# A hybrid trunk step: sums for the FFN's seven products formed ahead and in place, buffers kept through both FFN stages

## The chip, the cores and the metric

The kernel runs on one core of one Trainium2 chip. The time is that of one execution on the device, in microseconds (us), from three runs and one profiled execution. The engines of the core are TensorE (PE in the rows, its weight loads PEld), VectorE (DVE), ScalarE (ACT), GpSimd (POOL) and SyncE (SP), which issues nearly all DMAs. Each has its own queue of instructions, taken in order.

## The reference

One layer of a trunk: a token mixer (three head groups and one output projection), then a SwiGLU FFN, each with normalisation before and after. 2048 latent tokens and 256 context tokens pass, 1024 wide. The change touches the end of the mixer and the FFN; D_FF is 2816.

```python
def rmsnorm(x, g):
    y = xf * lax.rsqrt(jnp.mean(xf * xf, axis=-1, keepdims=True) + EPS)
    return (y * g.astype(jnp.float32)).astype(x.dtype)
...
    m, extra = mixer(h)
    x = x + gt1 * rmsnorm(m, g_norm[1])
    h = rmsnorm(x, g_norm[2]) * (1.0 + sc2) + sh2
    gate, up = jnp.split(h @ w_gu, 2, axis=-1)
    f = (jax.nn.silu(gate) * up) @ w_down
    x = x + gt2 * rmsnorm(f, g_norm[3])
```

## The kernel before

All matrices are fp32, and each product is made of three: an operand is split into a high part, rounded by ScalarE, and a low part, the rest, formed by VectorE (`split`, L1694 to L1696), and TensorE multiplies high by high, high by low and low by high. The 2304 tokens are 18 tiles of 128 (tiles 0 to 15 latent, 16 and 17 context) or six groups of 384.

**Output stage** (`phase_out`). For each tile TensorE makes the 48 matmuls of the output projection into `m`. Then come the residual (a ScalarE sum of squares L1671, two small GpSimd steps, VectorE L1673 and L1674) and the second norm (ScalarE L1606, VectorE `xn` L1608). `store` turns `xn` by eight transposes in four PSUM buffers `pst`, ScalarE evicts them with scale and shift (L1623), and a DMA writes them to `h2`. `store` of a tile comes two tiles later; the last two come after the loop. `ffn_ahead` loads the first operands of the FFN during the loop: the splits of two quarters of h (`hop0`, `hop1`), the raw half `hr1` and the first weights `wr0`.

**Up stage** (`ffn_up`). Three token blocks of 768 tokens, 22 units each. A unit makes 128 columns of gate and of up for a block. The 2 × 2 × 2 blocks (gate and up, two halves of the 1024 inputs, two token groups) are multiplied with seven products instead of eight, by sums of operands: products 1 and 2 add into PSUM buffer X, products 6, 7 and 4 into Y, 5 and 3 into Z. Each product is 12 matmuls of 128 × 384, so a unit has 84. `prep_h` forms the operands of h for a block, in two halves of 768 columns: four sums (two on VectorE, L1750 to L1758, two on GpSimd, L1762 and L1768) and the splits `hop`. `prep_w` loads the weights of a unit by three DMAs (`w_raw`), forms four sums S on GpSimd (L1786 to L1789) and splits seven operands `gop` from a pool of ten. Partial results leave X, Y and Z through ScalarE (`p1` L1809, silu L1826, L1831) and VectorE (`u2` L1814, `u3` L1820 and L1821, L1828, L1830); GpSimd makes the two last products (L1829, L1832), and six DMAs write `a`. TensorE runs the end of a unit (products 4 and 3) after the first product of the next.

**Down stage** (`ffn_down`). Two halves of 512 output columns, each 18 tiles of 22 row blocks with three matmuls of 128 × 512. `a_load` reads and splits half a tile's `a` (raw `ar`, split `ao`, three buffers each), `w_load` the 22 weight blocks (raw `wr`, four buffers; split `wd`, 24). All its buffers are opened when those of the up stage are closed. In each half the weights are loaded row by row while tile 0 runs.

**Order.** TensorE runs in the order of the code (`InOrder`, L31 to L42), and so does SyncE in the output stage. The order on VectorE, ScalarE, GpSimd, and SyncE in the FFN, is set by the tile scheduler, by priority and by when buffers come free.

## Time and profile before

| | us |
|---|---|
| three runs | 3836.85, 3842.79, 3843.37 |
| median | 3842.79 |
| profiled execution | 3837.47 |
| its span | 3835.5 |
| TensorE busy | 3607.6 (94%) |
| VectorE busy | 2308.8 (60%) |
| ScalarE busy | 1723.1 (45%) |
| GpSimd busy | 966.3 (25%) |

Busy times are sums over the span. The output stage ends at 2217 us, the up stage at 3251 us, and the down stage lasts to the end. The mean granted TensorE clock of the span is 0.974 of full. Line numbers are those of the kernel before; a name such as `hop` stands for all buffers of that name, and what was read stands right of `<-`.

### The profile page before, as it was taken

The page shows a single profiled execution, that of the slowest core. Times are in us where ns is not written, and L with a number is a line of the kernel's source. Part 1 is how long each engine was busy: PE and PEld are TensorE (multiplying, and loading weights), DVE is VectorE, ACT ScalarE, POOL GpSimd, SP SyncE. Part 2 cuts the span into 40 slices and gives each one's busy share as a digit, 9 for nine tenths or more (in the row PEclk, how much of TensorE's full clock was granted, in tenths as well). Part 3 has the DMA queues.
Part 4 walks back from the last instruction along what each step waited for, and adds up shares of the span by engine and source line. Part 5 has one row for each costly group of instructions (what it writes and reads, how often), then busy time and mean ns, then how long its engine had stood idle before and what let it go on. Part 6 is the DMA issues. An engine that isn't in the chain of part 4 may idle for free. (4 is left out here: it accounts for less than half of the span.)

```text
span 3835.5 us, 64839 instructions
## 1 busy us (share of the span) xinstructions
PE 3607.6 (94%) x24526; PEld 3166.5 (83%) x24526; DVE 2308.8 (60%) x4786; ACT 1723.1 (45%) x3552; POOL 966.3 (25%) x1135
## 2 busy tenths in 40 slices
PE   8997999969999999989999969999999998899999
PEld 5887988956777777778878869999999998688787
DVE  4784477689655555568765576677667664322433
ACT  4223322236666666657865643343334333322221
POOL 0002322620000000000003355556555553000111
PEclk9998999989999999999999989999999999899999
DMA  7565877741211112255325643333333332633654
GB/s 270 200 210 175 259 223 225 197 116 48 55 48 51 44 46 52 64 160 144 90 79 186 213 132 99 98 108 108 105 93 97 101 96 75 208 111 125 194 187 133
DMA packets 649081, 501.15 MB, mean 131 GB/s; under 512 B 253681, under 2 KB 577120, under 8 KB 646464
## 3 DMA queue, kind: packets, MB, share of 16 engines
q1 hardware_dynamic: 645984, 493.41, 42.9%
q8 instruction: 193, 3.16, 0.4%
q10 hardware_dynamic: 2624, 3.55, 0.3%
q14 instruction: 120, 0.98, 0.1%
q0 software_dynamic: 160, 0.05, 0.0%
HBM read 348.14 MB, written 148.73 MB: 130 GB/s over the span
## 5 line engine op out<-in xcount | busy, mean ns | idle before, releaser
L37 PE MATMUL pd<-wd,ao 128*128 128x512 f32 x2376 | 550.3, 394 | 26.1 <-DMA wr<-in_w_down_dram 15.0
L37 PEld LDWEIGHTS pd<-wd,ao 128*128 128x128 f32 x2376 | 450.6, 190 | 125.7 <-ACT ao L1695 15.4
L37 PE MATMUL Y<-hop,gop 128*128 128x384 f32 x2376 | 452.3, 338 | 22.4 <-ACT hop L1695 9.8
L1034 ACT ACTIVATE PT<-pt 128x512 f32<-128x512 f32 (+1 forms) x600 | 331.9, 553 | 256.3 <-PE pt L37 249.4
L37 PEld LDWEIGHTS Y<-hop,gop 128*128 128x128 f32 x2376 | 422.1, 191 | 24.2 <-ACT hop L1695 10.1
L1696 DVE TENSOR_TENSOR gop<-S,gop 128x512 fp32r<-128x512 f32 x264 | 235.6, 893 | 167.3 <-ACT gop L1695 157.6
L37 PE MATMUL X<-hop,gop 128*128 128x384 f32 x1584 | 306.2, 342 | 18.7 <-DVE hop L1696 8.9
L37 PE MATMUL po<-PT,V 128*64 128x256 f32 (+1 forms) x3072 | 313.5, 341 | 2.2 <-ACT PT L1034 1.9
L37 PE MATMUL pso<-whi,hi 128*128 128x384 f32 (+2 forms) x864 | 288.8, 334 | 25.3 <-ACT whi L255 13.8
L37 PEld LDWEIGHTS X<-hop,gop 128*128 128x128 f32 x1584 | 283.5, 190 | 20.8 <-DVE hop L1696 9.6
L37 PE MATMUL pt<-ident,P 128*128 128x128 f32 x1752 | 284.9, 280 | 14.9 <-ACT PT L1034 7.9
L37 PE MATMUL Z<-hop,gop 128*128 128x384 f32 x1584 | 297.7, 336 | 0.0
L37 PE MATMUL pso<-whi,lo 128*128 128x384 f32 (+2 forms) x864 | 282.6, 327 | 7.6 <-DMA lo<-hl 7.6
L37 PE MATMUL pso<-wlo,hi 128*128 128x384 f32 (+2 forms) x864 | 282.9, 327 | 0.8 <-DVE wlo L256 0.5
L37 PEld LDWEIGHTS Z<-hop,gop 128*128 128x128 f32 x1584 | 278.7, 189 | 0.1
L37 PEld LDWEIGHTS pt<-ident,P 128*128 128x128 f32 x1752 | 200.3, 141 | 94.4 <-ACT PT L1034 36.3
L1695 ACT ACTIVATE gop<-S 128x512 fp32r<-128x512 f32 x264 | 166.2, 630 | 228.2 <-PE Y L37 124.9
L971 POOL TENSOR_TENSOR rSe<-rS,eh 64x128 f32<-64x128 f32 x144 | 55.0, 400 | 811.6 <-DVE rS L1003 780.9
L1696 DVE TENSOR_TENSOR gop<-wr,gop 128x512 fp32r<-128x512 f32 x198 | 200.9, 1015 | 83.8 <-ACT gop L1695 77.6
L37 PEld LDWEIGHTS po<-PT,V 128*64 128x64 f32 x3072 | 180.4, 136 | 79.3 <-issue 33.7
L1695 ACT ACTIVATE gop<-wr 128x512 fp32r<-128x512 f32 x198 | 125.2, 632 | 245.3 <-PE Z L37 174.7
L1696 DVE TENSOR_TENSOR ao<-ar,ao 128x1408 fp32r<-128x1408 f32 x72 | 127.4, 1769 | 145.1 <-ACT ao L1695 143.1
(323 smaller groups left out, 7208.1 us busy)
## 6 DMA issues: line engine op xcount, KB each, us to landing
ar<-a SPq DMA_DIRECT2D x72, 704.0 KB, 4.8
wr<-in_w_gu_dram SPq DMA_DIRECT2D x66, 512.0 KB, 4.1
wr<-in_w_gu_dram SPq DMA_DIRECT2D x132, 256.0 KB, 3.4
a<-o SPq DMA_DIRECT2D x396, 64.0 KB, 2.1
wm<-in_w_mod_dram SPq DMA_DIRECT2D x48, 512.0 KB, 4.1
hi<-hh SPq DMA_DIRECT2D x36, 512.0 KB, 5.4
lo<-hl SPq DMA_DIRECT2D x36, 512.0 KB, 6.4
st<-ptk SPq DMA_DIRECT2D x18, 768.0 KB, 4.1
```

The lines of the kernel that those rows point to most:

```text
L37: r = f(*x, **kw)
L971: nc.gpsimd.tensor_tensor(Se[hh[x], d], S[hh[x], d, :, hh[x]], e.unsqueeze(2).to_broadcast([64, 2, 64]), ALU.mult)
L1034: self.nc.scalar.activation(out, p, AF.Copy)
L1695: self.nc.scalar.activation(hi, raw, AF.Copy)
L1696: self.nc.vector.tensor_tensor(lo, raw, hi.bitcast(F32), ALU.subtract)
```

## The change

The sums of h for the first block are formed in the output stage (`ffn_ahead`, tiles 12 to 15), in whole width (1536 columns) and in place: `ht` and the two halves of `hr1`. The first two weight operands are split at tiles 16 and 17. The last tile's norm goes into a kept buffer (`xn_last`), and its transposes, evictions and store move into the first unit, behind product 5. The weight sums S go from GpSimd to VectorE (`w_sums`). The weight operands use eight buffers, six of tag `raw` and two of tag `y` of the pool `o_p`, which now stays open through both FFN stages; `feed` makes an operand as soon as the product eight before has been issued. At a change of block each h operand is replaced, in place, behind its last product in the block's last unit (`h_put`), in one split of 1536 columns; the sums for the next block are written in units 12 to 16 of the running one (`ahead`). Products of a unit after the first run in the order 1, 6, 5, 2, 7, 4, 3, as before.

For the down stage, `feed` goes on with eight operands of w_down in the same buffers; two halves of `a` are loaded into the halves of `hr1` and split into the buffers of `ht` and `hop0`. A ring of four (`ht`, the two of `hop0`, one more) holds the `a` operands after that, two raw buffers feed it. Tiles 0 and 1 of each half run as a pair, row by row; the weights for the second half are loaded row by row while the last tile of the first half runs. All pools of the FFN release buffers tile by tile. `phase_out` has two buffers for transposes and shares two more, which the up stage and the first pair of down use after it.

```diff
+            pst = es.enter_context(tc.tile_pool(name="o_t", bufs=2, space=PSUM))
             psm = es.enter_context(tc.tile_pool(name="o_m", bufs=2, space=PSUM))
-            pst = es.enter_context(tc.tile_pool(name="o_t", bufs=4, space=PSUM))
+            banks = [pst, self.xps]
...
-                xn = nt[t] = wk.tile([128, 1024], F32, tag="xn", name="xn", bufs=3)
-                sq = wk.tile([128, 1024], BF16, tag="sq2", name="sq2", bufs=1)
+                xn = self.raw() if t == NT - 1 else wk.tile([128, 1024], F32, tag="xn", name="xn", bufs=3)
+                nt[t] = xn
...
-            store(NT - 1)
+            self.xn_last = nt.pop(NT - 1)
...
+        self.ht = pool.tile([128, 2, 4, BT], F32, name="ht", tag="ht")
+        self.fe = pool
...
             self.w_raw(0, self.wr0)
+            tt(self.ht[:, 0], self.hr1[:, 0:4], hop[:, 0].bitcast(F32), ALU.subtract)
+        if t == 13:
+            tt(self.ht[:, 0], self.ht[:, 0], hop[:, 1].bitcast(F32), ALU.subtract)
+        if t in (14, 15):
+            self.h_sums(t - 13)
+        if t >= NT - 2:
+            n = t - NT + 2
+            self.gops[0, n + 1] = self.g_op(self.wr0[:, n + 1])
+    def h_sums(self, i):
+        tt = self.nc.vector.tensor_tensor
+        B12, B22 = self.hr1[:, 0:4], self.hr1[:, 4:8]
+        if i == 1:
+            tt(self.ht[:, 1], B22, self.ht[:, 0], ALU.subtract)
+        else:
+            tt(B12, B22, B12, ALU.subtract)
...
+        x = self.yraw() if self.gn % 8 < 2 else self.raw()
+        self.gn += 1
+        return x.bitcast(F32R).rearrange("p (s x) -> p s x", s=2)
+    def g_op(self, x):
+        w = self.g_buf()
+        self.split(w[:, 0], w[:, 1], x)
+        return w
...
-            gp = es.enter_context(tc.tile_pool(name="u_g", bufs=10))
-            rp = es.enter_context(tc.tile_pool(name="u_r", bufs=2))
...
+            H = {n: hp.tile([128, 2, 4, BT], F32R, name=f"hop{n}") for n in (6, 5, 7, 4, 3)}
...
+            def h_load(tb, j):
+                self.sp.dma_start(hx, self.h2_d[2 * tb][:, 4 * j:4 * j + 4])
+            def h_put(tb, n):
+                if n == 4:
+                    tt(ht[:, 1], hx, ht[:, 1], ALU.subtract)
+                x = {1: hx, 2: hx, 3: hr1[:, 4:8], 4: ht[:, 1], 5: ht[:, 0], 6: ht[:, 1], 7: hr1[:, 0:4]}[n]
+                self.split(H[n][:, 0], H[n][:, 1], x)
+                if n == 1:
+                    h_load(tb, 1)
...
+            def w_sums(u):
+                A21, A11, A12, A22 = [wr[u % 2][:, i] for i in range(4)]
+                S = [wk.tile([128, 512], F32, tag="S", name="S", bufs=4) for _ in range(4)]
+                tt(S[0], A21, A22, ALU.add)
+                tt(S[1], S[0], A11, ALU.subtract)
+                tt(S[2], A11, A21, ALU.subtract)
+                tt(S[3], A12, S[1], ALU.subtract)
+                return {1: A11, 6: S[1], 5: S[0], 2: A12, 7: S[2], 4: A22, 3: S[3]}
+            made, done, raws = [2], set(), {}
...
+                    elif m >= 8 and m - 8 not in done:
+                        return
...
+                    if u >= NU:
+                        if self.down_feed(m - 7 * NU):
+                            return
...
-                gp_.tensor_tensor(S[0], A21, A22, ALU.add)
-                gp_.tensor_tensor(S[1], S[0], A11, ALU.subtract)
-                gp_.tensor_tensor(S[2], A11, A21, ALU.subtract)
-                gp_.tensor_tensor(S[3], A12, S[1], ALU.subtract)
-                for n, x in ((1, A11), (6, S[1]), (5, S[0]), (2, A12), (7, S[2]), (4, A22), (3, S[3])):
-                    put(n, x)
...
+                        n = ORD(u)[i]
+                        if n == 1 and u:
+                            raws[u] = w_sums(u)
+                        self.gops[u, n] = self.g_op(raws[u][n])
+                        if i == 6 and u + 2 < NU:
+                            self.w_raw((u + 2) % NF, wr[u % 2])
+                    made[0] += 1
...
+                if f == NF - 1 and tb < 2:
+                    h_put(tb + 1, n)
...
+                if u == 0:
+                    mm(X, u, 2, False, True)
+                    h_put(0, 6)
+                    feed(3)
+                    h2_last = self.raw()
...
+                    self.h2_store(NT - 1, self.xn_last, h2_last,
+                                  lambda: self.xps.tile([128, 512], F32, tag="pst", name="pst"))
+                    h_put(0, 7)
+                    feed(5)
...
+                    h_load(0, 1)
+                    h_put(0, 4)
+                    h_put(0, 3)
+                    feed(8)
...
+                if tb == 2:
+                    if f == 10:
+                        self.down_early()
+                        for t in range(2):
+                            self.d_raw(t, 0)
+                    elif f == 14:
+                        self.d_split()
+                    return
+                if f == 12:
+                    h_load(tb + 1, 0)
+                    self.sp.dma_start(hr1, self.h2_d[2 * tb + 3])
+                elif f == 14:
+                    tt(ht[:, 0], hr1[:, 0:4], hx, ALU.subtract)
+                elif f in (15, 16):
+                    self.h_sums(f - 14)
...
+        self.d_ops = [x.rearrange("p a b c -> p (a b c)")[:, :2816].rearrange("p (s c t) -> p s c t", s=2, c=11)
+                      for x in (ao, *self.hop0)]
+        self.d_raws = [self.hr1[:, 4 * i:4 * i + 4].rearrange("p a b -> p (a b)")[:, :1408]
+                       .rearrange("p (c t) -> p c t", c=11) for i in range(2)]
...
+    def w_op(self, n, c, w):
+        raw = self.wr0[:, self.d_n[2] % 4]
+        self.d_n[2] += 1
+        self.sp.dma_start(raw, self.a["w_down"][0, 128 * c:128 * c + 128, 512 * n:512 * n + 512])
+        self.split(w[:, 0], w[:, 1], raw)
+        self.d_w[n, c] = w
+    def down_feed(self, c):
+        if c >= 8:
+            return True
+        self.w_op(0, c, self.g_buf())
+        if c == 1:
+            self.d_split()
+            self.d_raw(0, 1)
+        elif c == 4:
+            self.d_split()
+            self.d_raw(1, 1)
...
+                self.w_op(n, c, self.g_buf() if n <= c < n + 8 else
+                          wp.tile([128, 2, 512], F32R, tag="wd", name="wd", bufs=15))
...
+                for ts in [(0, 1)] + [(t,) for t in range(2, NT)]:
...
+                            if ts[0] == 0:
+                                w_next(n, k)
+                            for t in ts:
+                                for i, (u, m) in enumerate(((0, 0), (0, 1), (1, 0))):
+                                    self.pe.matmul(p[t], lhsT=x[t][:, u, c], rhs=self.d_w[n, k][:, m],
+                                                   start=(k == 0 and i == 0), stop=(k == NF - 1 and i == 2),
+                                                   skip_group_check=True)
+                            if n == 0 and ts[0] == NT - 1 and k + 1 < NF:
+                                w_next(1, k)
```

Three places in the queues. First VectorE at the end of the output stage (`xn_26545` before and `raw_26556` after are the last tile's norm), before and after:

```order
L1673 SCALAR_TENSOR_TENSOR m_26466<-m_26466,rsr_26540,gt_24274 128x1024
L1674 TENSOR_TENSOR raw_26401<-raw_26401,m_26466 128x1024
L1608 TENSOR_SCALAR xn_26545<-raw_26401,o2r_26551 128x1024
L1750 TENSOR_TENSOR ht_26639<-hr1_24173,hop0_24171 128x768
L1751 TENSOR_TENSOR ht_26639<-ht_26639,hop0_24171 128x768
L1758 TENSOR_TENSOR ht_26642<-hr1_24173,ht_26639 128x768
L1696 TENSOR_TENSOR gop_26687<-wr0_24174,gop_26687 128x512
L1696 TENSOR_TENSOR gop_26690<-S_26680,gop_26690 128x512
L1696 TENSOR_TENSOR gop_26693<-S_26679,gop_26693 128x512
L1696 TENSOR_TENSOR gop_26696<-wr0_24174,gop_26696 128x512
```

```order
L1684 SCALAR_TENSOR_TENSOR m_26477<-m_26477,rsr_26551,gt_24278 128x1024
L1685 TENSOR_TENSOR raw_26409<-raw_26409,m_26477 128x1024
L1617 TENSOR_SCALAR raw_26556<-raw_26409,o2r_26562 128x1024
L1791 TENSOR_TENSOR S_26626<-wr0_24178 128x512
L1792 TENSOR_TENSOR S_26627<-S_26626,wr0_24178 128x512
L1793 TENSOR_TENSOR S_26628<-wr0_24178 128x512
L1794 TENSOR_TENSOR S_26629<-wr0_24178,S_26627 128x512
L1742 TENSOR_TENSOR hop6_26619<-ht_24177,hop6_26619 128x1536
L1742 TENSOR_TENSOR raw_26668<-S_26627,raw_26668 128x512
```

The weight sums S and one whole split of hop6 stand after the last norm, where three sums of h and the first weight split stood. On ScalarE, in the first unit of the up stage, before and after (`p1` is the eviction of X, `raw` and `y` with a source S or wr0 are weight operands, L1672 and L1623 the evictions of transposes):

```order
L1695 ACTIVATE gop_26687<-wr0_24174 128x512
L1695 ACTIVATE gop_26690<-S_26680 128x512
L1695 ACTIVATE gop_26693<-S_26679 128x512
L1695 ACTIVATE gop_26696<-wr0_24174 128x512
L1695 ACTIVATE gop_26699<-S_26681 128x512
L1695 ACTIVATE gop_26702<-wr0_24174 128x512
L1695 ACTIVATE gop_26705<-S_26682 128x512
L1695 ACTIVATE hop6_26635<-ht_26642 128x768
L1695 ACTIVATE hop5_26634<-ht_26639 128x768
L1695 ACTIVATE hop7_26636<-ht_26648 128x768
L1695 ACTIVATE hop3_26632<-hr1_24173 128x768 x2
L1809 ACTIVATE p1_26723<-X_26708 128x384
```

```order
L1615 ACTIVATE sq2_26557,s2_26558<-raw_26409 128x1024
L1672 ACTIVATE raw_26568<-pst_26569,b2_235,s2_234 128x128 x4
L1672 ACTIVATE raw_26568<-pst_26578,b2_235,s2_234 128x128 x4
L1741 ACTIVATE hop6_26619<-ht_24177 128x1536
L1741 ACTIVATE raw_26668<-S_26627 128x512
L1741 ACTIVATE hop5_26620<-ht_24177 128x1536
L1741 ACTIVATE raw_26688<-S_26626 128x512
L1741 ACTIVATE hop7_26621<-hr1_24176 128x1536
L1840 ACTIVATE p1_26652<-X_26637 128x384
L1741 ACTIVATE hop3_26623<-hr1_24176 128x1536
L1882 ACTIVATE sg_26844<-X_26637 128x384
L1741 ACTIVATE hop4_26622<-ht_24177 128x1536
```

Before, seven weight splits and five half splits of h stand ahead of p1; after, three whole h splits and two weight splits. At the change from block 0 to 1, VectorE, from the first half of hop6's replacement on, up to the eviction u3 of the last unit of block 0 or the first unit of block 1:

```order
L1696 TENSOR_TENSOR hop6_26635<-ht_29763,hop6_26635 128x768
L1814 TENSOR_TENSOR u2_29677<-Y_29611,p1_29663 128x384
L1756 TENSOR_TENSOR ht_29782<-hr1_24173 128x768
L1696 TENSOR_TENSOR hop5_26634<-ht_29756,hop5_26634 128x768
L1696 TENSOR_TENSOR gop_29831<-S_29813,gop_29831 128x512
L1758 TENSOR_TENSOR ht_29789<-hr1_24173,ht_29782 128x768
L1696 TENSOR_TENSOR hop1_24172<-hr4_26638,hop1_24172 128x768
L1696 TENSOR_TENSOR hop5_26634<-ht_29782,hop5_26634 128x768
L1696 TENSOR_TENSOR hop7_26636<-ht_29769,hop7_26636 128x768
L1820 TENSOR_TENSOR u3_29715<-Y_29611,p1_29663 128x384
```

```order
L1742 TENSOR_TENSOR hop6_26619<-ht_24177,hop6_26619 128x1536
L1742 TENSOR_TENSOR raw_29680<-S_29638,raw_29680 128x512
L1782 TENSOR_TENSOR ht_24177<-hx_26624,ht_24177 128x1536
L1742 TENSOR_TENSOR hop5_26620<-ht_24177,hop5_26620 128x1536
L1742 TENSOR_TENSOR raw_29699<-wr0_24178,raw_29699 128x512
L1742 TENSOR_TENSOR hop1_24175<-hx_26624,hop1_24175 128x1536
L1742 TENSOR_TENSOR raw_29716<-S_29640,raw_29716 128x512
L1742 TENSOR_TENSOR hop7_26621<-hr1_24176,hop7_26621 128x1536
L1742 TENSOR_TENSOR raw_29733<-wr0_24178,raw_29733 128x512
L1874 TENSOR_TENSOR u3_29736<-Y_29589,p1_29606 128x384
L1792 TENSOR_TENSOR S_29792<-S_29791,wr1_26625 128x512
L1875 TENSOR_TENSOR u3_29736<-Z_29590,u3_29736 128x384
```

Before, the rows split the first and second halves of the operands and form two sums; after, they replace whole operands between weight splits, ahead of u3. The nine rows ahead of these are hop0's replacement (1536), three weight splits, two sums S and three evictions (p1, u2 twice). At the end of the up stage, VectorE (S_35848 is the last weight sum; u3_35979 and u3_35925 belong to the last unit):

```order
L1696 TENSOR_TENSOR gop_35871<-S_35848,gop_35871 128x512
L1820 TENSOR_TENSOR u3_35839<-Y_35735,p1_35787 128x384
L1821 TENSOR_TENSOR u3_35839<-Z_35736,u3_35839 128x384
L1828 TENSOR_TENSOR p1_35787<-Y_35735,p1_35787 128x384
L1830 TENSOR_TENSOR u2_35801<-Z_35736,u2_35801 128x384
L1814 TENSOR_TENSOR u2_35941<-Y_35875,p1_35927 128x384
L1820 TENSOR_TENSOR u3_35979<-Y_35875,p1_35927 128x384
L1821 TENSOR_TENSOR u3_35979<-Z_35876,u3_35979 128x384
L1828 TENSOR_TENSOR p1_35927<-Y_35875,p1_35927 128x384
L1830 TENSOR_TENSOR u2_35941<-Z_35876,u2_35941 128x384
L1696 TENSOR_TENSOR wd_36066<-wr_36064,wd_36066 128x512
L1696 TENSOR_TENSOR wd_36074<-wr_36072,wd_36074 128x512
```

```order
L1742 TENSOR_TENSOR hop0_24174<-hr1_24176,hop0_24174 128x1408
L1742 TENSOR_TENSOR raw_35831<-wr0_24178,raw_35831 128x512
L1886 TENSOR_TENSOR u2_35737<-Z_35652,u2_35737 128x384
L1742 TENSOR_TENSOR raw_35835<-wr0_24178,raw_35835 128x512
L1851 TENSOR_TENSOR u2_35872<-Y_35788,p1_35802 128x384
L1742 TENSOR_TENSOR y_35868<-wr0_24178,y_35868 128x512
L1742 TENSOR_TENSOR y_35886<-wr0_24178,y_35886 128x512
L1742 TENSOR_TENSOR hop1_24175<-hr1_24176,hop1_24175 128x1408
L1742 TENSOR_TENSOR raw_35902<-wr0_24178,raw_35902 128x512
L1742 TENSOR_TENSOR raw_35921<-wr0_24178,raw_35921 128x512
L1874 TENSOR_TENSOR u3_35925<-Y_35788,p1_35802 128x384
L1875 TENSOR_TENSOR u3_35925<-Z_35789,u3_35925 128x384
```

Before, the first split of w_down (wd) comes after all evictions of the last unit; after, six splits of w_down and two of `a` (from hr1) stand ahead of its u3.

## Rows read from the trace of the kernel before

**Rows 1.** The chain that ended last, by line (page, part 4)
```profile
PE pd L37 13%; PE Y L37 10%; PE X L37 7%; PE Z L37 7%; PE m L37 2%; DMA wr<-in_w_down_dram 1%; DVE hop L1696 1%; DVE gop L1696 1%; PE pst L37 0%; DVE wd L1696 0%; ACT wd L1695 0%; DMA ar<-a 0%; ACT hop L1695 0%; ACT ao L1695 0%; DVE ht L1758 0%
```

**Rows 2.** Busy us by stretch: length, PE, PEld, DVE, ACT, POOL, clock, DMA, GB/s
```profile
2150.00:2200.00 50.00, 50.00 (x255) 42.11 (x254) 25.71 (x33) 29.82 (x76) 19.69 (x35) 1.00 0.59 189
2217.20:2270.00 52.80, 23.13 (x98) 20.79 (x97) 43.40 (x36) 27.94 (x55) 30.95 (x20) 0.68 0.51 152
2300.00:2350.00 50.00, 50.00 (x289) 50.00 (x288) 31.60 (x42) 19.63 (x35) 28.63 (x22) 1.00 0.31 91
2571.00:2615.00 44.00, 35.40 (x180) 34.66 (x179) 42.74 (x43) 19.89 (x32) 29.55 (x18) 0.88 0.47 135
2908.00:2941.00 33.00, 24.71 (x116) 24.07 (x115) 28.93 (x31) 15.57 (x25) 16.72 (x10) 0.84 0.32 92
3243.40:3300.00 56.60, 33.73 (x117) 25.04 (x117) 25.17 (x32) 21.32 (x31) 2.00 (x2) 0.76 0.68 228
3300.00:3350.00 50.00, 50.00 (x222) 41.39 (x221) 13.22 (x11) 11.86 (x15) 0.00 (x0) 1.00 0.50 163
3562.00:3575.00 13.00, 9.13 (x30) 6.39 (x30) 4.08 (x7) 5.73 (x9) 0.92 (x3) 0.87 0.47 163
```

**Rows 3.** PE timeline, out to up: start, us, engine, line, tiles, count [idle before <-releaser]
```profile
2217.18 1.91 PE L37 MATMUL pst<-ident,xn 128*128 128x128 f32 x16
...
2234.89 3.57 PE L37 MATMUL X<-hop,gop 128*128 128x384 f32 x10 [4.11 <-DVE gop L1696]
2241.50 3.69 PE L37 MATMUL X<-hop,gop 128*128 128x384 f32 x12 [3.04 <-ACT p L1809]
...
2256.02 0.69 PE L37 MATMUL Y<-hop,gop 128*128 128x384 f32 x1 [9.78 <-ACT hop L1695]
```

**Rows 4.** Timeline of all engines in the same stretch, three rows
```profile
2223.24 2.53 ACT L1623 ACTIVATE raw<-pst,b,s 128x128 f32<-128x128 f32 x7
...
2227.21 2.07 DVE L1750 TENSOR_TENSOR ht<-hr,hop 128x768 f32<-128x768 f32 x1 [2.18 <-PE pst L37]
...
2243.48 0.95 DVE L1750 TENSOR_TENSOR ht<-hr,hop 128x768 f32<-128x768 f32 x1
```

**Rows 5.** PE timeline at the change from block 0 to 1
```profile
2579.43 3.69 PE L37 MATMUL Y<-hop,gop 128*128 128x384 f32 x12 [3.99 <-DVE u L1820]
...
2597.34 1.97 PE L37 MATMUL X<-hop,gop 128*128 128x384 f32 x5 [4.61 <-DVE hop L1696]
```

**Rows 6.** PE timeline, up to down, and the second half of down
```profile
3265.80 1.22 PE L37 MATMUL pd<-wd,ao 128*128 128x512 f32 x2 [15.03 <-DMA wr<-in_w_down_dram]
...
3565.21 4.83 PE L37 MATMUL pd<-wd,ao 128*128 128x512 f32 x12 [2.99 <-ACT wd L1695]
```

**Rows 7.** Groups in 2300 to 2550 (up): count | busy us, mean ns | idle before
```profile
L1696 DVE TENSOR_TENSOR gop<-S,gop 128x512 fp32r<-128x512 f32 x69 | 57.6, 835 | 50.3 <-ACT gop L1695 47.5
L1696 DVE TENSOR_TENSOR gop<-wr,gop 128x512 fp32r<-128x512 f32 x51 | 51.5, 1009 | 24.0 <-ACT gop L1695 22.2
L1695 ACT ACTIVATE gop<-S 128x512 fp32r<-128x512 f32 x69 | 43.5, 631 | 59.6 <-PE Y L37 34.2 <-PE X L37 25.4
...
L1786 POOL TENSOR_TENSOR S<-wr 128x512 f32<-128x512 f32 x17 | 21.9, 1291 | 55.9 <-DVE gop L1696 55.9
...
L1814 DVE TENSOR_TENSOR u<-Y,p 128x384 f32<-128x384 f32 x17 | 9.3, 546 | 0.8 <-PE Y L37 0.8
```

**Rows 8.** Groups in 3300 to 3550 (down), columns as above
```profile
L1696 DVE TENSOR_TENSOR ao<-ar,ao 128x1408 fp32r<-128x1408 f32 x33 | 53.6, 1625 | 92.2 <-ACT ao L1695 92.2
L1695 ACT ACTIVATE ao<-ar 128x1408 fp32r<-128x1408 f32 x33 | 45.4, 1377 | 86.5 <-PE pd L37 86.5
...
L1696 DVE TENSOR_TENSOR wd<-wr,wd 128x512 fp32r<-128x512 f32 x10 | 6.4, 686 | 3.7 <-ACT wd L1695 3.7
```

**Rows 9.** DMA issues: count, KB each, us to landing; w_gu (page), w_down (3250 to 3300)
```profile
wr<-in_w_gu_dram SPq DMA_DIRECT2D x66, 512.0 KB, 4.1
...
wr<-in_w_down_dram SPq DMA_DIRECT2D x26, 256.0 KB, 4.6
```

295 lines of the change are left out of this document (143 added, 152 removed).

## The prediction

> **What bounds the kernel now.** I read the chain of waits first [rows 1]: its costliest lines are TensorE's products of the two FFN stages, and waits hardly show in it. So the FFN goes at TensorE's pace, and what it can lose lies where TensorE stops. The busy table by stretches [rows 2] tells where that is. Inside the up stage TensorE is busy for 50.00 of 50 us with 289 products, 0.173 us each; a unit of 84 takes 14.5 us. Inside the down stage it is 222 products in 50 us, 0.225 us each. Five stretches differ, and I measure each by its loss: length less what its products take at those two paces.
> - Out to up, 52.8 us: 24 transposes (0.12 us, from 1.91 for 16 [rows 3]) and 74 products, 15.7 us; loss 37.1.
> - Block 0 to 1, 44 us: 180 products, 31.1 us; loss 12.9. Block 1 to 2, 33 us: 116 products, 20.1; loss 12.9.
> - Up to down, 56.6 us: 36 products at 0.173 and 81 at 0.225, 24.5; loss 32.1.
> - First to second half of down, 13 us: 30 products, 6.8; loss 6.2.
>
> Together 101.2 us, of which part is the clock: the granted share in these stretches is 0.68 to 0.88 against 1.00 outside, so products right after an idle stretch run at the lower of the two levels, 1.2 GHz. After 3.99 us of idling, twelve took 3.69 us where 2.08 is usual [rows 5]. Everything that the change does is worth what it makes of these five losses, less what it costs in the 66 units between.
>
> **The change part by part.** I write T for the end of the last output product, 2217.2.
>
> *Out to up.* Before, the first unit waits for sums of h in pieces, seven weight splits and the h splits in one VectorE queue; the longest stop is 9.78 us for hop6, first product of Y [rows 3]. After, the h sums lie in the output stage: four whole-width VectorE operations of 1536 columns. I have none of that width; 1408 columns take 1.63 us [rows 8], so 1.77 by proportion. VectorE is busy there for 25.7 of 50 us while TensorE is at 50.00 [rows 2], so that cover takes four of them and two weight splits, 0.69 each [rows 8]; with no cover they would cost 8.5 us. The last tile's residual and norm keep their place at the head of VectorE's queue (the order shows L1684, L1685, L1617 ahead of the weight sums), so only its transposes have moved. X's first product waits for the ScalarE evictions of the tile before, whose last seven end at T+8.6 [rows 4]. It runs to about T+12.5 at the lower clock. On ScalarE five splits stand ahead of the copy p1: three of 1536 (1.50 each, from 1.38 for 1408 [rows 8]) and two of 512 (0.63 [rows 7]), 5.8 us, so p1 is there at T+15.3 (9.0 + 5.8 + 0.49). The second X product, Y6 and Z5 then run to T+22.7, the transposes to T+23.7. Y7 needs a weight split queued behind eight evictions of 0.36 us (2.53 for seven [rows 4]), some 3 us: it starts near T+27, and with Y4, Z3 and the second unit's X behind their splits the unit ends near T+38.4. Its work is 96 products and 24 transposes, 19.5 us. Loss 19; 14 if the queue of splits moves up, 26 if Y7 waits for SyncE's load of h and hop4 too.
>
> *Weight sums from GpSimd to VectorE.* Four operations of 512 columns a unit, 0.69 each by the VectorE split of that width while GpSimd is idle [rows 8]. Before: 4 × 0.835 + 3 × 1.009 + 5 × 0.55 = 9.1 us a unit [rows 7]; with every split at 0.69 it would be 7.6, so 1.5 us come from GpSimd's company, which is 8.3 us a unit [rows 2]. Without its sums (4 × 1.29 [rows 7]) GpSimd has 3.1 left, which by proportion costs VectorE 0.6. After: 7.6 + 2.8 + 0.6 = 11.0 of 14.5, between 10.4 (no company) and 11.9 (all 1.5 stay). VectorE is still under TensorE's pace, so the units between cost nothing. The first sum of a unit waits for weights: 512 KB, landing 4.1 us after issue [rows 9]; going through the queue I find about 7.9 us between their issue and the need, and 2.4 us to spare for u2, the first eviction of a unit that another engine waits for. With that cover gone, each us is 66 us.
>
> Here a rule speaks against the change. The trace: with GpSimd adding beside it, a subtraction of 768 columns took 2.07 us, alone 0.95 [rows 4]; over whole units the surcharge is 1.5 us for 8.3 of GpSimd. The Trainium skill ("SBUF — State Buffer", Who interferes with whom) says that the port pair of VectorE and GpSimd is an exclusive lock, the loser stopping for the whole instruction, and that VectorE operations with both inputs in SBUF meet it. By that rule GpSimd's 3.1 us a unit could hold VectorE for as long: an estimated 13.5 of 14.5, no stall between, but some 2 us more at each block change, 3784 rather than 3780. The trace's average is far under it, and I keep the average.
>
> *Block changes.* Operands are replaced in place after their last product, by 1536-column splits. The sums for the next block move to units 2 to 4 of the block that runs, where VectorE has 3.5 us a unit to spare: nothing, with that cover (3.5 us a block without). In the order, between hop0's low half, which can start when the last unit's X1 is done, and u3 of that unit stand six operations of 1.77, nine of 0.69 and four evictions of 0.55: 19.0 us. In that time TensorE has seven products, 14.5 us, then Y4 waits for u3. Stall 4.5, to 6 with GpSimd's company; the products behind it lose 1.6 by the clock [rows 5], and the third and fourth operand 0.5 to 2 more. Loss 9.5 each, against 12.9; bounds 5 (VectorE gets ahead, as it has 3.5 us a unit) and 13 (nothing won). ScalarE has less than VectorE at every step and is not last.
>
> *Up to down.* Before, TensorE idles 15.03 us for w_down [rows 6], whose buffers come free only with the stage. After, eight w_down operands and the first halves of two tiles are made in the last units from kept buffers. What is late next is u3 of the last unit: it stands behind the second tile's split (ScalarE 1.38, VectorE 1.63), which waits for X2's end, and two w splits (1.37): 4.9 us after X2, where Y7 ends at 2.1. Stall 3, clock 1.5, 0.5 for the first product of the pair. The pair of tiles takes six products per w row, 1.35 us. Loads have four raw buffers: 4.6 us to land [rows 9] and 1.9 to split make 1.6 us a row, eight rows ahead; row 21 is wanted 28 us in and there at 23, so the pair doesn't starve. Loss 5, between 2 and 12 (loads at 2 us a row).
>
> *Halves of down.* The second half's w operands are made one by one while the last tile runs, 0.69 of VectorE per 0.68 us of products, the first ones early. Loss 0.5 (0 to 4), before 6.2 [rows 6]. The shared ring of four a operands needs two splits of 1.63 per 14.9 us tile. Pools that release by tile cost no instruction; I put them at nothing, and the wait that they add at the worst is that of the h splits, counted above.
>
> **Sum.** Losses after: 19 + 9.5 + 9.5 + 5 + 0.5 = 43.5; before 101.2; gain 57.7. The profiled execution took 3837.5 us (span 3835.5), so 3779.8; the median of the runs is 5.3 above it, and of that I add 2: 3782.
>
> **The rivals.**
> - *VectorE becomes the bound of a unit.* It now holds sums, splits and evictions in one queue. If the order makes it wait (the first sum for weights, u2 behind it, then Y7 for u2), each unit runs longer than 14.5 us. Against it: 11.0 of 14.5. For it: it waits in turn for weights, ScalarE and TensorE, and GpSimd can hold it. It decides from 57.7/66 = 0.87 us a unit, a period of 15.4. At 1.2 us: 3837.5 − 57.7 + 79 = 3859, with the 2 us 3861, slower.
> - *Only the down stage gains.* The first unit still waits for the last norm (its place has not changed) and VectorE's backlog at block changes only changes its make-up, so those three losses stay: the change doesn't do there what it says. Gain 27.1 + 5.7 = 32.8: 3807. For it: 19 us of VectorE in 14.5; against it: the 9.78 stop goes, as its sum is made beforehand.
> - *Nearly all is hidden.* VectorE runs ahead in its spare time: losses 14 + 5 + 5 + 2 + 0 = 26, gain 75: 3764.
> - *Gains given back in part*, 0.8 us a unit in the first rival's way: within 0.2%, about 7.7 us, which is about what a measurement of this kernel can tell from no change.
>
> **How the numbers follow.** Forecast 0.66, its own range 3769 to 3799; only the down stage 0.15; nearly all hidden 0.10; within 0.2% 0.04; slower 0.05. The range 3760 to 3808 takes in the first three cases but for part of their edges. Faster 0.91, same 0.04, slower 0.05.
>
> **What would show it.** In the changed kernel: TensorE busy at 0.173 us a product between the changes, with no stop that recurs each unit; VectorE's weight sums near 0.69 us and VectorE's busy time near 11 of each 14.5; GpSimd near 3; the first unit's longest stops before X2 (for p1) and Y7 (for a split on ScalarE), none near 9.8 us for hop6; one stop of 4 to 6 us for u3 at each block change; no stop over 5 us between up and down, and none for w_down; no 2.99 us stop at the second half. A stop for u2 or Y7 in every unit would prove the first rival; losses near 37 and 13 at the first three places the second.

## The result, and the profile of the kernel after

The changed kernel takes 3793.65 us (median of 4 runs, 3790.19 to 3797.81) against 3839.9 us for the kernel before on the same chip: 0.988 of it, with a 95% interval of 0.9863 to 0.9897. It is faster, by some 46 us. The profiled run took 3790.19 us with a span of 3788.4, against 3835.5 before: 47.1 us. The forecast was 3782, a gain of 57.7. The direction and the range were right; the size was 11 us too large. The reasons below show that this is two errors of opposite sign.

The busy table by stretches of the kernel after, the stretches laid around the same five places as in [rows 2], with one stretch inside each stage between them. Columns: window; its length, then busy us (and count) of PE, PEld, DVE, ACT and POOL; granted clock; DMA share; GB/s.

```profile
2218.50:2270.00 51.50, 39.36 (x212) 38.19 (x211) 44.51 (x58) 32.34 (x61) 5.51 (x7) 0.90 0.64 197
2350.00:2450.00 100.00, 100.00 (x573) 100.00 (x572) 74.11 (x111) 38.17 (x68) 17.12 (x14) 1.00 0.34 99
2540.00:2584.00 44.00, 38.62 (x208) 38.11 (x207) 38.24 (x47) 23.58 (x33) 5.29 (x4) 0.92 0.51 156
2880.00:2913.00 33.00, 27.62 (x147) 27.30 (x147) 30.60 (x37) 18.80 (x25) 5.29 (x4) 0.90 0.46 140
3210.00:3266.00 56.00, 52.05 (x238) 44.81 (x237) 31.83 (x38) 23.44 (x35) 5.55 (x4) 0.97 0.74 236
3350.00:3450.00 100.00, 100.00 (x433) 80.99 (x432) 25.33 (x20) 21.98 (x27) 0.00 (x0) 1.00 0.36 110
3500.00:3530.00 30.00, 30.00 (x131) 24.37 (x130) 16.09 (x21) 13.82 (x21) 0.00 (x0) 1.00 0.72 233
```

The same two 100 us stretches of the kernel before:

```profile
2350.00:2450.00 100.00, 100.00 (x576) 100.00 (x575) 60.49 (x83) 38.28 (x69) 53.31 (x41) 1.00 0.35 100
3350.00:3450.00 100.00, 100.00 (x443) 82.81 (x442) 27.27 (x21) 22.80 (x28) 0.00 (x0) 1.00 0.34 113
```

Two things are to be seen. First, the five places lost far less: with the prediction's own measure (length less products at 0.173 and 0.225 us), out to up 16.1 us (51.5 less 24 × 0.12 and 188 × 0.173), the block changes 8.0 and 7.6, up to down 6.5 (78 up products and 160 of down; 0.9 of that is the slower pace told next, so 5.6), the second half nothing beyond that pace. That is 37.3 instead of 101.2: 63.9 us gained. Second, where nothing stops, TensorE is 100% busy at a clock of 1.00 in both kernels, and yet issues fewer products in the same time: 573 instead of 576 in up, 433 instead of 443 in down. Over 5544 up products (66 units of 84) that is 5544 × (100/573 − 100/576) = 5.0 us; over 2376 down products 2376 × (100/433 − 100/443) = 12.4 us. 63.9 − 17.4 = 46.5, against 47.1 by the spans. (The counts are whole products, so each of the two paces is good to some 1.5 us.) A view of stops alone would never show the 17.4: TensorE does not idle, each product takes longer.

The stops that remain at the first place, TensorE's timeline of the kernel after (start, us, engine, line, operation, tiles, count, idle before and its releaser); the last row is the first block change, which repeats at 2895.72 with the same 5.38, and at the hand-over to down (3223.27) with 3.95:

```profile
2227.52 3.89 PE L37 MATMUL X<-hop,y 128*128 128x384 f32 x12 [7.09 <-ACT raw L1672]
2233.05 2.38 PE L37 MATMUL X<-hop,y 128*128 128x384 f32 x12 [1.64 <-ACT p L1840]
2243.77 4.27 PE L37 MATMUL Y<-hop,raw 128*128 128x384 f32 x12 [3.30 <-ACT raw L1741]
...
2564.35 4.21 PE L37 MATMUL Y<-hop,y 128*128 128x384 f32 x12 [5.38 <-DVE u L1874]
```

The 9.78 for hop6, the 15.03 for w_down and the 2.99 at the second half [rows 3, 6] are gone. What is left in the blocks is one stop for u3, as forecast. The stretches 2350 to 2450 show what moved between engines: GpSimd's (POOL's) share falls from 53.3 to 17.1 us per 100, VectorE's (DVE's) grows from 60.5 to 74.1, which is 10.9 us of a 14.66 us unit.

### The profile page after: what moved, and what is told of

The parts are those of the page before. It is cut to its first block, busy times and chain, and to the rows that moved or that the text cites. A ratio compares the mean times of both kernels' runs of the same rounds, so it can differ in the third digit from the quotient of the medians.

```text
span 3788.4 us, 64737 instructions
## 1 busy us (share of the span) xinstructions
PE 3601.8 (95%) x24526; PEld 3157.9 (83%) x24526; DVE 2398.9 (63%) x5030; ACT 1718.5 (45%) x3533; POOL 590.5 (16%) x859
## 4 chain that ended last, share of the span: by engine, by line
PE 74%; DVE 11%; ACT 4%; POOL 4%; DMA 3%; issue 3%; SPq 1%; ACTq 0%; DVEq 0%; POOLq 0%
PE pd L37 15%; PE Y L37 11%; PE pso L37 8%; PE X L37 7%; PE Z L37 7%; PE pt L37 7%; PE po L37 6%; PE rx L37 3%; DVE stmp L843 2%; PE Sa L37 2%; PE Sb L37 2%; PE S L37 2%; DVE mx L1220 2%; PE m L37 1%; DVE sW L844 1%
## 5 line engine op out<-in xcount | busy, mean ns | idle before, releaser
L37 PE MATMUL Y<-hop,raw 128*128 128x384 f32 x1788 | 341.5, 340 | 12.7 <-DVE u L1874 9.3
L37 PEld LDWEIGHTS Y<-hop,raw 128*128 128x128 f32 x1788 | 317.8, 190 | 14.1 <-DVE u L1874 10.0
L37 PE MATMUL Z<-hop,raw 128*128 128x384 f32 x1188 | 224.1, 337 | 0.0
L37 PE MATMUL X<-hop,raw 128*128 128x384 f32 x1176 | 222.9, 338 | 0.0
L1742 DVE TENSOR_TENSOR raw<-S,raw 128x512 fp32r<-128x512 f32 x198 | 146.8, 742 | 115.5 <-ACT raw L1741 110.5
L37 PEld LDWEIGHTS Z<-hop,raw 128*128 128x128 f32 x1188 | 209.6, 188 | 0.0
L37 PEld LDWEIGHTS X<-hop,raw 128*128 128x128 f32 x1176 | 208.4, 188 | 0.0
L37 PEld LDWEIGHTS pso<-whi,hi 128*128 128x128 f32 x864 | 166.7, 193 | 31.8 <-ACT whi L255 16.5
L37 PE MATMUL pd<-wd,ao 128*128 128x512 f32 x756 | 185.5, 394 | 0.0
L37 PE MATMUL pd<-wd,hop 128*128 128x512 f32 x756 | 183.0, 392 | 0.0
```

Source lines behind the costliest of these rows:

```text
L37: r = f(*x, **kw)
L1742: self.nc.vector.tensor_tensor(lo, raw, hi.bitcast(F32), ALU.subtract)
```

## The experiments

All kernels compute everything. Ratios are to runs of the kernel before made alongside, with their 95% intervals. The question with the most time in it came first: why does a product take longer, at the same clock and with the same work?

**Operands aligned.** The build of a kernel gives the start address of each buffer in its partition. After the change the operands start at other addresses than before, some at odd multiples of 32 bytes. The first theory: starts off 64 bytes are slow. One kernel gives every operand of the kernel after a 64-byte start (a longer `fss` or an unused buffer ahead; a small scratch buffer of the output stage is shared to make room), the other moves down's operands of the kernel before by 32 bytes, all together.

```diff
+        pool.tile([128, 8], F32, name="pad")
...
-            ss = cst.tile([128, 2, NT], F32, name="fss")
+            ss = cst.tile([128, 2, 24], F32, name="fss")
```

> The changed kernel with 32 bytes of padding at the head of o_p, 32 at the end of f_e and a longer fss, so that every operand of both FFN stages begins at a multiple of 64 bytes; in the changed kernel all operands of the up stage and all w operands of the down stage begin 32 bytes behind such a multiple, and of the a operands of the down stage three buffers of four (to make room, one small scratch of the output stage is shared). Theory 1, the address of an operand sets TensorE's pace: down 0.2308 to about 0.2265 us a product (2376 of them, 10 us), up 0.1744 to about 0.173 (5544, 4 to 8 us); 12 to 18 us faster than the changed kernel, some 3777. Rival, the pace comes with the new structure (kept buffers of several kinds, pairs of tiles, release by tile): both paces stay, change within 3 us.

> The kernel before with one scratch tile of the down stage (fss) 48 bytes longer, which moves all w and a operands of that stage from multiples of 64 bytes to 32 bytes behind them; nothing else moves. Theory 1 (address): down 0.2257 to 0.229 to 0.231 us a product, 8 to 12 us slower than before, the up stage as it was. Rival (structure): pace 0.2257 as it was, within 2 us of before.

The first measured 0.9881 (0.9866 to 0.9896; 3794.09 us), the second 1.0 (0.999 to 1.0009; 3839.25 us). The stretches 2350 to 2450 and 3350 to 3450 of the aligned kernel first, then 3350 to 3450 of the kernel before with the shift:

```profile
2350.00:2450.00 100.00, 100.00 (x576) 100.00 (x575) 73.00 (x109) 38.56 (x68) 16.11 (x13) 1.00 0.35 101
3350.00:3450.00 100.00, 100.00 (x431) 80.67 (x431) 25.33 (x20) 21.98 (x27) 0.00 (x0) 1.00 0.37 111
```

```profile
3350.00:3450.00 100.00, 100.00 (x443) 82.81 (x442) 25.57 (x20) 22.43 (x28) 0.00 (x0) 1.00 0.35 115
```

Aligned operands stay slow in down, and misaligned ones stay fast when both move together: the theory falls. But the aligned kernel did bring the up stage back to 576 products per 100 us, so addresses do matter. What the kernel before and its shifted copy have in common in down is the distance between the start of the moving operand (512 columns) and that of the stationary one (128 × 128): zero modulo 512 bytes in both, and 64, 128 or 352 in the kernel after. In up the aligned kernel moved it for X alone, from 384 to 320, and X's products are what became faster; Y and Z stayed at 448. That distance, here called the offset, is the second theory, and the next three kernels test it.

**Equal offsets.** Unused buffers shift the operands of the kernel after so that, for every product of the FFN, moving and stationary operand start at the same address modulo 512 bytes. In the output stage a scratch buffer is shared to make room.

```diff
+        pool.tile([128, 96], F32, name="pad")
...
+            hp.tile([128, 80], F32, name="pad")
...
+            wp.tile([128, 80], F32, name="pad")
...
-            ss = cst.tile([128, 2, NT], F32, name="fss")
+            ss = cst.tile([128, 2, 64], F32, name="fss")
```

> The changed kernel with pads in f_e, in u_h and in the pools of the down stage, so that the moving and the stationary operand of every product of the FFN begin at addresses that are equal modulo 512 bytes (to make room, two scratch tiles of the output stage share a buffer). In the kernel before this holds for all products of the down stage and for those of Y and Z (hop3 to hop7); in the changed kernel for none. Theory 2, the offset between the two operands' addresses sets TensorE's pace, not the address of either: down 0.2317 to 0.2268 us a product, up 0.1752 to 0.1736; 18 to 21 us faster than the changed kernel, some 3774. Rival (structure): both paces stay, change within 3 us.

Measured: 3768.59 us, 0.9814 (0.9799 to 0.9829), about 25 us less than the kernel after (0.0066 of 3840).

```profile
2350.00:2450.00 100.00, 100.00 (x578) 100.00 (x578) 74.81 (x112) 38.59 (x68) 17.14 (x14) 1.00 0.34 99
3350.00:3450.00 100.00, 100.00 (x443) 82.81 (x442) 25.34 (x20) 23.03 (x28) 0.00 (x0) 1.00 0.38 115
```

Down is back at 443, and up at 578 is faster than it was before the change. At those paces 8.4 us come from up and 12.4 from down, 20.8 of the 25; in this run the output stage was also 3.9 us shorter than in that of the kernel after (232.9 us from its first to its last product, instead of 236.8). That is spread between runs: the kernel with late evictions moved ahead, below, has the same output stage and took 236.2, and the kernel before and its three copies with moved operands, which are alike up to down, took 236.1 to 238.8.

**The same cost put into the kernel before.** One unused buffer ahead of down's a operand moves it by 384 bytes (offset 128 modulo 512) in one kernel, by 256 in another. Nothing else differs.

```diff
+                wk.tile([128, 96], F32, name="pad", tag="pad", bufs=1)
```

> The kernel before with one unused tile of 384 bytes ahead of the a operands of the down stage, which makes the offset between w and a operands 128 modulo 512 instead of 0; nothing else moves. Theory 2: down pace 0.2268 to 0.2326 us a product, as the products of the changed kernel that have this offset, 13 to 14 us slower than before. Rival (structure): the pace stays 0.2268, within 2 us of before.

> The kernel before with one unused tile of 256 bytes ahead of the a operands of the down stage: offset between w and a operands 256 modulo 512, nothing else moved. If the period of theory 2 is 512 bytes: pace above 0.2268, between 0.229 and 0.2335 us a product as at the other offsets seen (64, 128, 352), 5 to 16 us slower than before. If the period is 256 bytes or less: pace 0.2268, within 2 us of before.

The first measured 3856.45 us, 1.0038 (1.0024 to 1.0052): some 15 us slower by doing nothing but moving an operand. The second measured 3841.01 us, 0.9997 (0.9988 to 1.0007). The down stretch of the two:

```profile
3350.00:3450.00 100.00, 100.00 (x432) 81.10 (x431) 25.98 (x20) 22.00 (x27) 0.00 (x0) 1.00 0.34 113
```

```profile
3350.00:3450.00 100.00, 100.00 (x442) 82.81 (x442) 26.16 (x21) 23.38 (x28) 0.00 (x0) 1.00 0.34 113
```

So the offset is the cause of down's slower pace, and 256 bytes count as zero there.

**Only the up side of the change.** The kernel after with the down stage of the kernel before: its pools, its loads, no operands made ahead.

```diff
-        if c >= 8:
+        if c >= 0:
             return True
...
-                    if f == 10:
-                        self.down_early()
...
-            wp = es.enter_context(tc.tile_pool(name="d_w", bufs=1, reuse_waits="tile"))
+            wp = es.enter_context(tc.tile_pool(name="d_w", bufs=2))
```

> The changed kernel up to the end of the up stage, and then the down stage of the kernel before (its pools opened when those of the up stage are closed, nothing of w_down or a made ahead). Theory of the forecast: the stop of some 15 us for w_down returns, 26 us of loss more at the hand-over and 6 at the second half, while the pace of the products returns to 0.2268 with the old buffers, 12 us less: 18 to 23 us slower than the changed kernel, some 3814. Rival (the hand-over is hidden by what the scheduler moves ahead): less than 8 us slower.

Measured: 3812.47 us, 0.9927 (0.9912 to 0.9942), 18 us above the kernel after by the ratios. TensorE's timeline at the hand-over shows the old stop back; the down pace (443 per 100 us) is the old one too, and a stop of 2.3 us returns at the second half.

```profile
3245.53 1.22 PE L37 MATMUL pd<-wd,ao 128*128 128x512 f32 x2 [14.58 <-DMA wr<-in_w_down_dram]
...
3540.17 0.49 PE L37 MATMUL pd<-wd,ao 128*128 128x512 f32 x1 [2.32 <-ACT wd L1741]
```

So the changed down stage was worth 18 us net; with the 12.4 that its operands' offsets cost, some 30. Forecast for it was 32.8 (27.1 and 5.7).

**The last norm turned early**, as in the kernel before, with all else of the change.

```diff
-            self.xn_last = nt.pop(NT - 1)
+            store(NT - 1)
...
-                    self.h2_store(NT - 1, self.xn_last, h2_last,
```

> The changed kernel with the last tile's norm turned at the end of the output stage again (eight transposes and eight evictions ahead of the first unit's products). Theory of the forecast: the late turn by itself is worth little, since X waits for the evictions of the tile before in any case; the second X product comes 1 to 2 us later, and the stop of 3.3 us ahead of Y7, where the weight split is queued behind the eight evictions, goes: within 4 us of the changed kernel on either side. Rival (the late turn is where the first unit gained): 5 us or more slower.

Measured: 3797.53 us, 0.9887 (0.9872 to 0.9901). The interval overlaps that of the kernel after, so the 3.9 us between the medians is not settled by the times. TensorE's timeline shows the mechanism: it now waits for the norm itself. The stop ahead of Y7 is gone, as expected, but the next unit's X waits as long for a weight split (3.52). From the last output product to the first product of down it is 1011.7 us, against 1010.8 in the kernel after, so the late turn by itself is worth little.

```profile
2234.61 1.94 PE L37 MATMUL pst<-ident,raw 128*128 128x128 f32 x8 [6.09 <-DVE raw L1617]
2242.34 3.81 PE L37 MATMUL X<-hop,y 128*128 128x384 f32 x12 [2.32 <-ACT p L1840]
2256.42 3.52 PE L37 MATMUL X<-hop,raw 128*128 128x384 f32 x10 [3.52 <-DVE raw L1742]
```

**u3 moved ahead.** In the last unit of a block the two operations of u3 get priority over the splits for the next block. One theory has only u3's place in VectorE's queue at fault; the rival has VectorE late as such, so that the stop only moves.

```diff
+                with ExitStack() as pr:
+                    if f == NF - 1:
+                        pr.enter_context(tc.high_priority(offset=40))
-                tt(u3, Y, p1, ALU.add)
+                    tt(u3, Y, p1, ALU.add)
```

> The changed kernel with a higher priority for the two additions that write u3 in the last unit of each block, so that on VectorE they stand behind hop5's replacement and ahead of those of hop1 and hop7 (in the last block: directly behind the split of a into hop1). Theory: u3 is what TensorE waits for at the three places (5.38, 5.38 and 3.95 us, and some 2 us of lower clock behind each): the stops fall below 1 us at the block changes, to about 2.5 at the hand-over to down; 13 to 17 us faster. Rival: VectorE is late as such, so the next operand (hop1, hop7, hop4) is waited for instead, with 3 to 5 us at the same places: under 5 us faster in all.

Measured: 3787.69 us, 0.9868 (0.9853 to 0.9882), hardly to be told from the kernel after. TensorE's timeline: the stop for u3 is nearly gone, and one product group of the next unit waits for u2 instead.

```profile
2562.99 2.36 PE L37 MATMUL Y<-hop,y 128*128 128x384 f32 x12 [0.24 <-DVE u L1877]
...
2578.25 4.21 PE L37 MATMUL Y<-hop,raw 128*128 128x384 f32 x12 [4.49 <-DVE u L1851]
```

So at the block changes the stop only moves, as the rival had it: whichever eviction stands behind the splits and sums is waited for. That VectorE is late as such does not follow from it, as the run that moves u2 too shows below. At the hand-over to down, the stop for u3 falls from 3.95 to 1.50 us.

**Weight sums back on GpSimd**, with all else of the change.

```diff
-                tt(S[0], A21, A22, ALU.add)
+                gt = nc.gpsimd.tensor_tensor
+                gt(S[0], A21, A22, ALU.add)
```

(and the other three alike)

> The changed kernel with the four weight sums of a unit on GpSimd again, all else kept. Theory of the forecast (the sums are covered on either engine between the block changes; on VectorE they only lengthen its row ahead of u3): no stop inside the units, 0.1744 us a product as it is; at the block changes two sums and one sum of h leave the row ahead of u3 (3.1 us) and GpSimd's company lengthens the splits there by 1 to 2 us: stops of 3.5 to 4.5 instead of 5.4; the first unit 1 to 2 us later, as its sums take 1.3 us each; in all 0 to 4 us faster. Rival (moving the sums is where the change gained): 5 us or more slower, with stops for weight operands in the units.

Measured: 3808.99 us, 0.9921 (0.9906 to 0.9936): about 15 us slower than the kernel after, where I expected the same or a little faster. The pace in up is unchanged (573), so the time is in stops. TensorE's timeline, out to up and first block change:

```profile
2251.62 4.30 PE L37 MATMUL Y<-hop,raw 128*128 128x384 f32 x12 [6.91 <-ACT raw L1741]
...
2578.33 3.69 PE L37 MATMUL Y<-hop,y 128*128 128x384 f32 x12 [6.34 <-DVE u L1875]
2591.86 2.39 PE L37 MATMUL Y<-hop,raw 128*128 128x384 f32 x12 [1.48 <-DVE u L1852]
2608.06 2.36 PE L37 MATMUL Y<-hop,raw 128*128 128x384 f32 x12 [1.27 <-DVE u L1852]
```

VectorE and GpSimd in the same block change of this kernel, two rows each:

```profile
2565.94 2.28 DVE L1742 TENSOR_TENSOR hop<-ht,hop 128x1536 fp32r<-128x1536 f32 x1 [1.51 <-ACT hop L1741]
...
2570.41 1.79 DVE L1742 TENSOR_TENSOR raw<-wr,raw 128x512 fp32r<-128x512 f32 x1
```

```profile
2568.96 2.70 POOL L1793 TENSOR_TENSOR S<-S,wr 128x512 f32<-128x512 f32 x1 [2.35 <-issue]
2574.55 2.71 POOL L1794 TENSOR_TENSOR S<-wr 128x512 f32<-128x512 f32 x1 [2.90 <-DVE raw L1742]
```

The split that runs beside the first sum takes 1.79 us, where 0.68 is usual, and the sum 2.70 where [rows 7] has means of 0.8 to 1.3 us for VectorE's and GpSimd's operations of 512 columns. Both lose, just where VectorE is already late. But this is the smaller part. Counted from the last output product, this kernel is 8.8 us behind the kernel after when three units are done, and the two block changes add some 5 us together, of 15.2 at the end of up. In the first unit ScalarE's queue stands still for GpSimd's sum for the second unit, with the evictions of the last transposes and the split for Y7 behind it:

```profile
2243.49 1.15 ACT L1741 ACTIVATE y<-S 128x512 fp32r<-128x512 f32 x2 [4.88 <-POOL S L1793]
```

How much of that lateness is GpSimd's own time for a sum, and how much is lost by running beside VectorE, this run doesn't separate. No weight operand is waited for in the later units: the rival was right on the size, and on its reason in the first unit alone.

**Both late evictions moved ahead, with equal offsets.** Since u3 alone moved the stop, this kernel (off0u) gives priority to u2 and u3, in a block's last unit and in the first two units of later blocks, on top of the equal offsets.

```diff
+                    if f == NF - 1 or tb and f < 2:
+                        pr.enter_context(tc.high_priority(offset=40))
```

> The kernel with equal offsets (off0), and a higher priority for the additions u2 and u3 in the last unit of a block and, in the later blocks, in the first two. Theory (VectorE is late as such at a block change, and only the order in which it is late can be chosen): u3 and u2 are no longer waited for, a split is, stops of 2 to 4 us within two units instead of 5.4 to 5.9; with 2 us less at the hand-over to down, 4 to 9 us faster than off0. Rival (TensorE waits for these two evictions and for nothing behind them): 13 us or more faster.

Measured: 3753.47 us, 0.9774 (0.976 to 0.9789): 15 us less than with equal offsets alone, and the fastest kernel of the study. TensorE's timeline has these stops left at the first block change and the hand-over, where equal offsets alone left 5.52 and 4.22:

```profile
2554.11 2.37 PE L37 MATMUL Y<-hop,y 128*128 128x384 f32 x12 [0.38 <-DVE u L1882]
2569.85 2.37 PE L37 MATMUL Y<-hop,raw 128*128 128x384 f32 x12 [0.89 <-DVE u L1882]
...
3197.91 2.37 PE L37 MATMUL Y<-hop,raw 128*128 128x384 f32 x12 [1.52 <-DVE u L1882]
```

The rival held: TensorE waits for these two evictions and for nothing behind them, and the theory that VectorE is late as such falls. Its splits for products 3 to 7 of the next block have room, the two evictions have none.

**Out to up reordered, on top of that** (best2). The transposes get other PSUM buffers, so that X's first product need not wait for the last evictions; the second X product and the last norm move behind Z's first.

```diff
-                    mm(X, u, 2, False, True)
...
                     feed(5)
+                    mm(X, u, 2, False, True)
+                    self.h2_store(NT - 1, self.xn_last, h2_last,
```

> off0u, and three edits at out to up: the two PSUM pools of the output stage change places, so that the first X lies in a bank of m that has long been free instead of one of the last transposes; the second X product comes behind product 5; the last tile's transposes and evictions come behind the split for Y7. Theory (X waits 7.1 us for the evictions of transposes, Y7 3.1 us for ScalarE): X at 2 instead of 9 us behind the last output product, Y6 at 13 instead of 17, no stop for Y7; 4 to 8 us faster than off0u. Rival (the chain through the last norm and the weight sums on VectorE is as late): under 2 us.

Measured: 3754.68 us, 0.9777 (0.9763 to 0.9792): no gain. X's first product starts 2 us after the output stage, but Y6 then waits for its weight split on ScalarE and, one product on, for the low half of hop6 on VectorE, and X later waits again. TensorE's rows, then VectorE's split of hop6:

```profile
2226.28 0.69 PE L37 MATMUL Y<-hop,raw 128*128 128x384 f32 x1 [6.87 <-ACT raw L1742]
2227.55 4.17 PE L37 MATMUL Y<-hop,raw 128*128 128x384 f32 x11 [0.58 <-DVE hop L1743]
...
2243.19 0.62 PE L37 MATMUL X<-hop,raw 128*128 128x384 f32 x2 [3.33 <-ACT raw L1742]
2245.31 3.57 PE L37 MATMUL X<-hop,raw 128*128 128x384 f32 x10 [1.50 <-DVE raw L1743]
```

```profile
2225.74 1.76 DVE L1743 TENSOR_TENSOR hop<-ht,hop 128x1536 fp32r<-128x1536 f32 x1
```

The 7.09 wait was only the first in line. ScalarE's split comes behind the last evictions, and VectorE's split of hop6 behind the last norm and the four weight sums, which run without a gap from 2222.48 on. Both chains end within 1.3 us of each other, as the rival had it.

**One sum of h per block change on GpSimd, on top of that**, to relieve VectorE by 1.75 us.

```diff
-                    tt(ht[:, 1], hx, ht[:, 1], ALU.subtract)
+                    (nc.gpsimd.tensor_tensor if tb else tt)(ht[:, 1], hx, ht[:, 1], ALU.subtract)
```

> best2 with one of the sums of h at a block change (that for hop4) on GpSimd, which is idle for most of a unit, instead of VectorE. Theory (VectorE's backlog is what is waited for): 1.75 us less ahead of u3 at each change, less what GpSimd's company adds to the splits (0.6 to 1.2 us): 1 to 4 us faster than best2. Rival (GpSimd's company costs as much as it saves): within 1 us, or slower.

Measured: 3765.51 us, 0.9802 (0.9786 to 0.9819): about 10 us slower, with the stop for u3 back at 4.30 us. GpSimd's and VectorE's rows at the change:

```profile
2556.30 3.97 POOL L1784 TENSOR_TENSOR ht<-hx,ht 128x1536 f32<-128x1536 f32 x1
```

```profile
2553.72 1.75 DVE L1743 TENSOR_TENSOR hop<-ht,hop 128x1536 fp32r<-128x1536 f32 x1
2555.39 1.50 DVE L1743 TENSOR_TENSOR raw<-S,raw 128x512 fp32r<-128x512 f32 x1
2556.81 5.07 DVE L1743 TENSOR_TENSOR hop<-ht,hop 128x1536 fp32r<-128x1536 f32 x1
```

The split beside GpSimd's sum took 5.07 us instead of 1.75: 3.3 us lost of a 3.97 us company, to save 1.75.

## Why the prediction was right and where it was wrong

**Out to up: right.** Loss 16.1 against a forecast of 19 (14 to 26). The order of the stops was as worked out: X's first product behind the last evictions, the second behind p1 (1.64), Y7 behind a ScalarE split (3.30). Each of them is ScalarE's work, on which the working rested. The last reordering shows a second chain right behind it, VectorE's through the last norm and the weight sums.

**Block changes: mechanism right, a little too dear.** One stop for u3 of 5.38, forecast 4.5 to 6; losses 8.0 and 7.6 against 9.5. The stop comes from u3's place in VectorE's queue, as the working had it. The forecast took that place as given. Moving u3 alone leaves VectorE's next eviction late, but with u2 and u3 both ahead the stops are 0.4 to 1.5 us: an order exists that hides nearly all of it, which at these places would have been the rival "nearly all is hidden".

**Up to down and second half: right.** 5.6 against 5, nothing against 0.5; the kernel with the old down stage brings the 15 us stop back and costs 18 us net. The rival "only the down stage gains" fell: the three other terms moved too.

**VectorE under TensorE's pace: right.** 10.9 us a unit against 11.0, no stop that recurs. In the stretch 2300 to 2550 of the kernel after, the four weight sums come to 3.47 us a unit instead of 2.8, two of them 0.69 as taken and two near 1.0. Instruction by instruction, the second of these two (L1794) takes 0.69 us in the 9 units where GpSimd is idle beside it and 1.39 in the 8 where one of its two products runs:

```profile
L1791 DVE TENSOR_TENSOR S<-wr 128x512 f32<-128x512 f32 x17 | 18.0, 1060 | 0.6
L1794 DVE TENSOR_TENSOR S<-wr,S 128x512 f32<-128x512 f32 x17 | 17.4, 1021 | 0.5
L1792 DVE TENSOR_TENSOR S<-S,wr 128x512 f32<-128x512 f32 x17 | 11.8, 692 | 0.6
L1793 DVE TENSOR_TENSOR S<-wr 128x512 f32<-128x512 f32 x17 | 11.8, 692 | 0.6
```

**The units between: wrong.** "The units between cost nothing" is the step that failed. It asked only whether an engine would make TensorE wait, and kept 0.173 and 0.225 us as constants of a product. They depend on where the operands lie, and the change, by new and longer-lived buffers, put them elsewhere: 17.4 us. The padded kernels show it for down both ways (taken out of the kernel after, put into the kernel before). For up, the kernel with equal offsets takes it out. There the change had moved Y and Z, from 0 to 448; X had 384 in both kernels, and with equal offsets it became faster than it was before the change. The trace of before could have hinted at it. In the build of before every product of X has an offset of 384, every one of Y and Z has none; and in its timeline the X groups take longer to the next start than the Y group (2.12 against 2.08 us):

```profile
2701.24 2.28 PE L37 MATMUL X<-hop,gop 128*128 128x384 f32 x12
2703.36 2.24 PE L37 MATMUL Y<-hop,gop 128*128 128x384 f32 x12
2705.44 2.28 PE L37 MATMUL X<-hop,gop 128*128 128x384 f32 x12
```

**GpSimd's company: the average was the wrong number where it counts.** The prediction weighed a rule against the trace's average surcharge of 1.5 us for 8.3 of GpSimd, and kept the average. In steady state that changed nothing, as VectorE has room there. Where VectorE is the late engine, single operations decide: 1.79 us instead of 0.68, and 5.07 instead of 1.75 beside 3.97 of GpSimd, which made one kernel about 5 us slower at each block change. The Trainium skill ("SBUF — State Buffer", Who interferes with whom) describes an exclusive lock, in which the loser stops for the whole instruction. These rows agree with it: the two long splits end 0.54 and 1.61 us after the GpSimd operation beside them, about what such splits take alone (0.68 and 1.75). The kernel with the sums on GpSimd is 15 us slower, so moving the sums away from GpSimd, which I had put down as a cost with little return, is a part of the gain. How much of the 15 us is the lock and how much GpSimd's own time for a sum stays open. My expectation for that run was wrong: it put 1 to 2 us on the first unit, where the first three lost 9, and shorter stops at the block changes, where they grew from 5.38 to 6.34.

In short: the stops came out 6 us better than forecast, the pace 17 us worse.

## What to carry to other kernels

Read the pace of a saturated engine as products per stretch, not only its stops; when buffers are moved, kept longer or renamed, compare the start addresses of the two operands of each product, and pad them equal where the pace has fallen. When one queue is late, first find the evictions that another engine waits for, all of them, and order those ahead; moving one may only move the stop. Before relieving a late VectorE by an operation on GpSimd beside it, count what both lose: here it cost 10 us to move one sum at each of two block changes.
